# Hybrid decoder step on one core: the output weights' sums split over three places, and the sample rows' products moved

## The chip, the cores and the metric

The kernel runs on one core of a Trainium2 chip. The engines named here are PE (TensorE, matrix products), DVE (VectorE), ACT (ScalarE), POOL (GpSimd) and SP (SyncE, which issues nearly all the DMAs of this kernel, in the order of its queue). The metric is the device time of one execution in microseconds (us); three runs of the kernel before took 834.67, 834.83 and 835.5 us, with the median 834.83.

## The reference

One layer of a decoder, applied to a prompt of 1024 rows of width 1024 and to 8 x 4 sample rows with their caches and states. Two branches read the same normalised input h: a matrix memory (mLSTM, 4 heads of 128) and a windowed attention with sinks (8 heads of 64). The branches are gated, projected, merged, projected once more, and added to x; a last RMSNorm ends it. What matters here is its end:

```python
def layer(x, c, C0, n0, m0, k_past, v_past, w_ada, b_ada, g_norm, w_in, ..., w_mo, w_ao, w_o):
    h, gate = adaln_in(x, c, w_ada, b_ada, g_norm)
    (mq, mk, mv, mi, mf, mo, mz, aq, ak, av, az, gm, ga) = split_in(h @ w_in)
    y_m, C, n, m = mlstm_branch(mq, mk, mv, mi, mf, mo, mz, C0, n0, m0, b_i, b_f, g_mn)
    ...
    y_a = o.astype(x.dtype) * jax.nn.silu(az)
    u = jax.nn.sigmoid(gm) * (y_m @ w_mo) + jax.nn.sigmoid(ga) * (y_a @ w_ao)
    x = x + gate * (u @ w_o)

y_prompt = rmsnorm(yp, g_final)
y_sample = rmsnorm(ys, g_final)
```

The other outputs are the new states and caches. w_o is the tensor w_out of the kernel; gate is one vector of 1024 for the whole prompt, so the kernel multiplies the columns of w_out by it once and leaves it out of the product of the prompt's rows.

## The kernel before

**Products.** A product in fp32 is made as three matmuls of a faster format: each operand is split into a high part (a cast, on ACT) and a low part (operand minus high part, on DVE), and `mm` (line 275) issues hi x hi, hi x lo and lo x hi. In the names a tile with h at its end, or wh, is a high part; l or wl is a low part. Large products are made by Strassen's scheme: two by two blocks, seven products of sums of blocks instead of eight. The sums are DVE work, and a split follows each.

**Stages.** The input and the projections; from about 205 to 650 us the 18 pairs of `block_products` (4 `head_in`, 8 `gate`, 2 `query_gate`, 4 `head_gate`, each pair seven products of two blocks); the attention's output product (tiles wl_ao.., ax, ay, u_h); the heads' output product `mem_out` (tiles g_w_mo, eight steps d of three pieces each, about 692 to 741 us); the output rows (four blocks of 256 rows, seven products each, tiles foX, foZ, foW and foY in PSUM); and a short tail. In a block of rows the products come in the order 1, 5, 6, 2, 7, 3, 4.

**Side work.** Beside the pairs run generators: the sample rows' heads, the prompt's heads, and `out_weights` (line 1964). They are held by a planner (`Side`) whose clock `side.now` is advanced by each matmul's estimated time; a generator yields a lag, and is stepped again when the clock has passed it. What a step issues goes to its engine's queue at that place. Each engine works its queue in order, so this planner and the order of the code set what stands ahead of what. In the output rows the order is that of the code.

**The output weights.** `out_weights` starts in the sixth pair. For each K tile of KA = (0, 1, 4, 5) it loads four raw tiles of w_out (wor), multiplies them by the gate (gb), makes the seven operands b11, b21, b22, t1, t2, t3, t4 of Strassen's scheme, splits each (wosh on ACT, wosl on DVE) and stores both parts to DRAM (woD). In `mem_out` the 28 pairs of parts are loaded again (wo_b11h, wo_b11l and so on, 256 KB each) by `weights_out`.

**The samples' last head.** Beside the `head_gate` pairs the last sample head ends in a chain of small DVE instructions, a reciprocal (fsden), a root by Newton steps (fsv, fsr_y, fsr_w) and a scaled tile sz. PE transposes sz into sty, and DVE makes gs of it.

**w_mo.** Each step d of `mem_out` needs the weight tile w_mo of that d: loaded by `preload` (wr_w_mo), split by ACT (wh_w_mo) and DVE (wl_w_mo). Behind a piece of PE's, DVE takes the result with a gate tile: tgw_mo<-tgw_mo,g_w_mo, then u_h or u_l<-u,tgw_mo. The splits of d + 1 are issued in the middle of the step d.

**The sample rows.** `sample_rows` is a generator that the output loop steps by `aside(...)`, which names the blocks in which that place takes a step. Its product of 32 sample rows with w_out is made in four groups of four small matmuls (tile fo in the profile, fo8_0 and fo8_1 in the code), each group reading four raw tiles of w_out that stand in rows_l and rows_h. The loads of the first group are issued ahead of the first product, behind g_final, gsD (the samples' gate, loaded twice into the same tile) and two tiles of x_prompt.

Of the kernel before, what the change touches and what calls it, by code (L numbers as in the profile page):

```python
# [24 lines left out]
NS = NB * NT  # L25
# [148 lines left out]
def body(tc, a):  # L174
    nc = tc.nc
    with ExitStack() as ctx:
# [17 lines left out]
        def ht(shape, name, dt=F32):  # L194
            return sp.tile(shape, dt, tag="half", bufs=50, name=name)
# [58 lines left out]
        def dma(out, in_, late=False):  # L254
            stores(in_.tensor)
            issue(out, in_, late)
# [1446 lines left out]
        def att_products():  # L1703
# [26 lines left out]
            for j, (n, i) in enumerate(flat):  # L1730
# [9 lines left out]
                if i == 3 and n == 2:  # L1740
                    split(ymD, *ymx, PCOLS, 0)
                if i == 2 and not nxt:
                    for d in range(2):
                        preload(("w_mo", d))
                split_ahead(j + 2)
                if i == 3 and not nxt:
# [216 lines left out]

        def out_weights():

            gb = [ht([128, 512], f"gb2{f}") for f in range(2)]
            for f in range(2):
                dma(gb[f], gbD[:, HALF[f]].to_broadcast((128, 512)))

            def keep(n, k, t):  # L1970
                parts = [ht([128, 512], f"wos{x}", F32R) for x in "hl"]
                S.copy(parts[0], t)
                V.tensor_tensor(parts[1], t, parts[0].bitcast(F32), op=ALU.subtract)
                woD[n, k] = [dp.tile([128, 512], F32, name=f"woD{n}{k}{x}") for x in "hl"]
                for d, x in zip(woD[n, k], parts):
                    due.append((side.now + 4.0, d, x.bitcast(F32)))

            for k in KA:
                raws = []
                for kk in (k, k + 2):  # L1980
                    for f in range(2):
                        raws.append(ht([128, 512], f"wor{k}{f}"))
                        dma(raws[-1], a["w_out"][kk * 128:(kk + 1) * 128, HALF[f]])
                yield 10.0, ""
                for j, t in enumerate(raws):
                    with not_before(V):
                        V.tensor_tensor(t, t, gb[j % 2], op=ALU.mult)
                    yield 2.4, ""
# [4 lines left out]
                yield WLAG, ""  # L1993
                V.tensor_tensor(b12, b12, b11, op=ALU.subtract)
                keep("t1", k, b12)
                yield WLAG, ""
                keep("b11", k, b11)
                yield WLAG, ""
                V.tensor_tensor(b11, b11, t3, op=ALU.add)
                keep("t2", k, b11)  # L2000
                yield WLAG, ""
                keep("t3", k, t3)
                yield WLAG, ""
                keep("b21", k, b21)
                yield WLAG, ""
                V.tensor_tensor(b21, b21, b11, op=ALU.subtract)
                keep("t4", k, b21)
                yield WLAG, ""

        KA, WLAG = (0, 1, 4, 5), 4.0  # L2010
        pairs = [Pair(head_in, i) for i in range(len(paired))] + [Pair(gate, d) for d in range(KT)] + [Pair(query_gate, i) for i in range(2)] + [Pair(head_gate, h) for h in range(NH)]

        def hook(n, i):
            if n == 0 and i in (6, 5):
                side.until(lambda: {6: "t2", 5: "t1"}[i] in formed)
            if i == 6:
                if pairs[n].kind is query_gate:
                    side.until(lambda: len(units_done) == 16)
                side.until(lambda: len(samples_done) >= {head_in: 0, gate: 0, query_gate: 1, head_gate: pairs[n].i + 2}[pairs[n].kind])
            if (n, i) == (OUT_WEIGHTS, 6):  # L2020
                side.add("g", out_weights())
            if (n, i) in LOADS:
                side.add("x", att_sums(LOADS.index((n, i))))
# [22 lines left out]
        for _ in att:  # L2046
            pass
        side.finish("x")
        banks[:] = [pg, pg, pa, pa]
        class Rows:  # L2050

# [26 lines left out]
            def product(self, n, o, first, c0=0, w=512):  # L2078
                hi, lo = self.w[n]
                for k in range(4):  # L2080
                    bh, bl = (t[:, c0:c0 + w] for t in wo[OPERANDS[n]][k])
# [5 lines left out]
        wo = {n: [] for n in ("b11", "b21", "b22", "t1", "t2", "t3", "t4")}  # L2087
# [8 lines left out]
        def weights_out(n):  # L2096
            for _ in range(n):
                n, k = wo_parts.pop(0)
                aside = len(wo_parts) < 8
                hi = ht([128, 512], f"wo_{n}h", F32R)  # L2100
                lo = granule(f"wo_{n}l", "wr", 9, F32R).rearrange("p k n -> p (k n)") if aside else ht([128, 512], f"wo_{n}l", F32R)
                for t, d in zip((hi, lo), woD[n, k]):
                    dma(t.bitcast(F32), d, True)
                wo[n].append((hi, lo))
# [50 lines left out]
        def sample_rows():  # L2155
# [14 lines left out]
            for f in range(2):  # L2170
# [34 lines left out]
        for i, r in enumerate(blocks_of_rows):  # L2205
# [35 lines left out]
            def seventh():  # L2241
# [114 lines left out]
```

## Time and profile before

| | us |
|---|---|
| median of three runs (834.67 to 835.5) | 834.83 |
| the profiled execution | 833.81 |
| its span in the profile | 832.0 |
| PE busy | 805.9 (97%) |
| DVE busy | 604.6 (73%) |
| ACT busy | 417.9 (50%) |
| POOL busy | 47.5 (6%) |

A row of a timeline gives the start, the duration, the engine, the line, the operation, then what is written and what is read by the program's names (without buffer numbers), shapes, and in brackets how long the engine stood idle before it and for what. Lines 220, 261, 275 and 280 are helpers through which all the work goes, so the tile names tell the places. A list of waits gives who waited for whom: total, times, longest. Durations of neighbouring rows overlap a little, since instructions are pipelined: two rows of 0.67 on DVE start 0.6 apart, and matmuls with 512 columns last 0.39 and start 0.23 apart. A row of windows gives the window, its length, the busy time of PE, PE's weight loads, DVE, ACT and POOL with their instruction counts, PE's granted clock (1.00 is full), the mean share of the DMA engines and GB/s. The mean granted clock of the whole execution is 0.995.

### The profile page before, as it was taken

How to read it: one execution, taken by the hardware profiler on the slowest of the kernel's cores; microseconds unless marked ns; L12 is line 12 of the kernel's file. 1: busy time of each engine (PE TensorE's matmuls, PEld its weight loads, DVE VectorE, ACT ScalarE, POOL GpSimd, SP SyncE). 2: the span in 40 equal slices, each digit the busy share in tenths (PEclk: the TensorE clock that was granted, in tenths of full speed). 3: DMA queues.
4: the chain of work that ended last, by engine and by line, in shares of the span. 5: the costliest groups of instructions: out<-in, count | busy, mean ns of one | idle time of the engine just before them, and what ended most of it. 6: DMA issues, size and time to landing. Idle time of an engine off the chain costs nothing.

```text
span 832.0 us, 15086 instructions
## 1 busy us (share of the span) xinstructions
PE 805.9 (97%) x5105; PEld 666.3 (80%) x5105; DVE 604.6 (73%) x1503; ACT 417.9 (50%) x1019; POOL 47.5 (6%) x111
## 2 busy tenths in 40 slices
PE   6999999999999999999999999998999999999996
PEld 3779797888788788888888778886888789987775
DVE  4889886747646456476656997999568996565887
ACT  5664366556455564555655555445346652014433
POOL 0120000000000001000001001101002101000000
PEclk9999999999999999999999999999999999999998
DMA  9995657446535325537756667768536789766632
GB/s 335 371 318 160 224 180 219 155 163 194 177 123 192 130 73 170 184 100 263 246 172 216 220 217 233 250 202 274 169 94 187 240 308 380 283 209 209 203 108 107
DMA packets 116481, 171.79 MB, mean 206 GB/s; under 512 B 21536, under 2 KB 55456, under 8 KB 116372
## 3 DMA queue, kind: packets, MB, share of 16 engines
q1 hardware_dynamic: 110756, 160.08, 58.2%
q10 hardware_dynamic: 4176, 6.56, 2.1%
q0 software_dynamic: 1472, 4.20, 1.4%
q8 instruction: 40, 0.66, 0.3%
q14 instruction: 37, 0.30, 0.1%
HBM read 118.13 MB, written 53.67 MB: 206 GB/s over the span
## 4 chain that ended last, share of the span: by engine, by line
PE 80%; DVE 11%; DMA 3%; issue 3%; ACT 2%; SPq 1%; DVEq 0%; ACTq 0%
PE bx L275 11%; PE bw L275 10%; PE by L275 10%; PE g_w_mo L275 6%; PE bz L275 5%; PE g_mq L275 3%; PE g_aq L275 3%; PE foX L275 2%; PE sc L275 2%; PE oT L275 2%; PE smp L275 2%; PE pt L280 2%; PE foW L275 2%; PE n L275 2%; PE g_mv L275 1%
## 5 line engine op out<-in xcount | busy, mean ns | idle before, releaser
L220 ACT ACTIVATE p<-p,nmx 128x256 f32<-128x256 f32 (+1 forms) x64 | 31.0, 486 | 18.7 <-DVE nmx L220 18.4
L275 PE MATMUL g_w_mo<-ym_l,wl_w_mo 128*128 128x384 f32 (+1 forms) x96 | 31.1, 324 | 2.4 <-DVE wl_w_mo L220 2.4
L275 PE MATMUL g_aq<-h_h,wh_aq 128*128 128x384 f32 (+1 forms) x96 | 32.2, 336 | 0.0
L275 PE MATMUL g_aq<-h_h,wl_aq 128*128 128x384 f32 (+1 forms) x96 | 30.9, 322 | 0.0
L275 PE MATMUL g_aq<-h_l,wh_aq 128*128 128x384 f32 (+1 forms) x96 | 30.8, 321 | 0.0
L275 PE MATMUL g_w_mo<-ym_l,wh_w_mo 128*128 128x384 f32 (+1 forms) x96 | 30.8, 321 | 0.0
L275 PE MATMUL g_w_mo<-ym_h,wh_w_mo 128*128 128x384 f32 (+1 forms) x96 | 30.8, 321 | 0.0
L220 DVE CUSTOM_DVE_ANT_0 p<-sc,cst,sink 128x256 f32<-128x256 f32 (+1 forms) x64 | 26.1, 462 | 5.3 <-PE sc L275 5.2
L220 DVE SCALAR_TENSOR_TENSOR tgw_mo<-tgw_mo,g_w_mo 128x384 f32<-128x384 f32 (+1 forms) x24 | 12.5, 520 | 19.7 <-PE g_w_mo L275 18.2
L275 PEld LDWEIGHTS g_w_mo<-ym_l,wl_w_mo 128*128 128x128 f32 x96 | 18.0, 188 | 3.4 <-DVE wl_w_mo L220 3.4
L275 PEld LDWEIGHTS g_aq<-h_h,wh_aq 128*128 128x128 f32 x96 | 18.0, 188 | 2.6 <-issue 1.5
L220 DVE TENSOR_TENSOR et<-et,S 128x384 f32<-128x384 f32 (+1 forms) x12 | 6.1, 509 | 19.2 <-PE S L275 16.4
L261 POOL DMA_DIRECT2D oD<-uqv x16 | 8.8, 552 | 184.3 <-ACT uqv L220 171.0
L220 DVE TENSOR_TENSOR wosl<-wor,wosh 128x512 fp32r<-128x512 f32 x24 | 16.5, 686 | 3.7 <-ACT wosh L220 3.0
L275 PE MATMUL sc<-ukv,uqv 64*128 64x256 f32 (+1 forms) x128 | 18.0, 390 | 0.7 <-DMA ukv<-kD 0.6
L275 PEld LDWEIGHTS g_w_mo<-ym_l,wh_w_mo 128*128 128x128 f32 x96 | 18.0, 188 | 0.0
L275 PEld LDWEIGHTS g_w_mo<-ym_h,wh_w_mo 128*128 128x128 f32 x96 | 18.0, 188 | 0.0
L275 PEld LDWEIGHTS g_aq<-h_l,wh_aq 128*128 128x128 f32 x96 | 18.0, 188 | 0.0
L275 PEld LDWEIGHTS g_aq<-h_h,wl_aq 128*128 128x128 f32 x96 | 18.0, 188 | 0.0
L220 ACT CAST wh_w_mo<-wr_w_mo 128x512 fp32r<-128x512 f32 x8 | 4.9, 622 | 26.1 <-DMA wr_w_mo<-w_mo 17.1
L220 DVE COPY p<-pt 128x512 f32<-128x512 f32 (+1 forms) x16 | 10.5, 655 | 10.3 <-PE pt L280 10.3
L220 ACT CAST wosh<-wor 128x512 fp32r<-128x512 f32 x24 | 14.9, 621 | 4.8 <-DVE wor L220 2.0
(1961 smaller groups left out, 2831.3 us busy)
## 6 DMA issues: line engine op xcount, KB each, us to landing
x<-xT SPq DMA_DIRECT2D x16, 256.0 KB
early_h<-w_ada SPq DMA_DIRECT2D x8, 512.0 KB
adar_ga<-w_ada SPq DMA_DIRECT2D x16, 256.0 KB
wr_ga<-w SPq DMA_DIRECT2D x16, 256.0 KB
wr_gm<-w SPq DMA_DIRECT2D x16, 256.0 KB
taD<-gt SPq DMA_DIRECT2D x16, 256.0 KB
tmD<-gt SPq DMA_DIRECT2D x16, 256.0 KB
wor<-w_out SPq DMA_DIRECT2D x16, 256.0 KB
```

The lines of the kernel that those rows point to most:

```text
L220: ins = f(*args, **kw)
L261: ins = (eng or nc.sync).dma_start(out, in_)
L275: in_order(nc.tensor.matmul(out, lhsT, rhs, start=start, stop=stop, skip_group_check=more))
L280: in_order(nc.tensor.transpose(out, in_, idn))
```

## The change

It has five parts.

1. `out_weights` treats the K tiles by place. Tiles 0 and 1 are made beside the heads as before. Tile 4 waits until the second `head_gate` pair has begun and, before it multiplies, until all the sample heads are done; its lags are 3.0 and not 4.0. Tile 5 waits until all the heads are finished, is made inside `mem_out`, and its parts stay on chip (`wo[n][5] = parts`): they are neither stored nor loaded.
2. `weights_out` loads 21 pairs of parts and not 28, on another schedule: (3, 3, 3, 2, 2, 1, 0, 0) behind the steps of `mem_out`, seven at the end. `out_weights` is finished in the last step of `mem_out` and not ahead of the first.
3. Four tiles of w_mo are loaded ahead of `mem_out` and not two, and each step d loads d + 4.
4. `sample_rows` multiplies its sums by the gate in the step in which they are added, with one yield fewer.
5. In the output loop the step behind product 6 is now taken in blocks 0, 1 and 2 and not only 1 and 2, and the step behind product 2 is gone.

```diff
@@ att_products
-                    for d in range(2):
+                    for d in range(4):
                         preload(("w_mo", d))
@@ out_weights
                 S.copy(parts[0], t)
                 V.tensor_tensor(parts[1], t, parts[0].bitcast(F32), op=ALU.subtract)
+                if k == KA[-1]:
+                    wo[n][k] = parts
+                    return
...
             for k in KA:
+                lag = WLAG
+                if k in KA[2:]:
+                    while len(begun) < k - 3:
+                        yield 1.0, ""
+                    lag = 3.0
+                if k != KA[1]:
+                    gb = [ht([128, 512], f"gb2{f}") for f in range(2)]
+                    for f in range(2):
+                        dma(gb[f], gbD[:, HALF[f]].to_broadcast((128, 512)))
...
                 yield 10.0, ""
+                while k == KA[2] and len(samples_done) < NH + 1:
+                    yield 0.5, ""
@@ hook
+            if n == len(pairs) - NH + 1 and not begun:
+                begun.append(4)
...
         side.finish("x")
+        begun.append(5)
@@ output weights and mem_out
-        wo_parts = [(n, k) for n in ("b11", "t1", "t2", "b21", "t3", "b22", "t4") for k in KA]
+        wo_parts = [(n, k) for n in ("b11", "t1", "t2", "b21", "t3", "b22", "t4") for k in KA[:3]]
...
-        side.finish("g")
         for d in range(KT):
             if d == KT - 1:
+                side.finish("g")
                 row_start()
+            elif d < KT - 4:
+                preload(("w_mo", d + 4))
             mem_out(d, ymx, u, row_start if d == KT - 1 else None)
-            if d < 6:
-                weights_out((4, 4, 4, 3, 3, 3)[d])
+            weights_out((3, 3, 3, 2, 2, 1, 0, 0)[d])
         weights_out(len(wo_parts))
@@ sample_rows
                     V.tensor_tensor(sums[f], acc[f][j:j + 32], sums[f], op=ALU.add)
-                yield
+                V.tensor_tensor(sums[f], sums[f], gsb[:NS, HALF[f]], op=ALU.mult)
+            yield
             for f in range(2):
-                V.tensor_tensor(sums[f], sums[f], gsb[:NS, HALF[f]], op=ALU.mult)
                 V.tensor_tensor(xb[:NS, HALF[f]], xb[:NS, HALF[f]], sums[f], op=ALU.add)
@@ the output loop
-            aside(1, 2)
+            aside(0, 1, 2)
             for c in range(2) if i else ():
                 rows_out(2 * i - 2 + c, before[0][c], rs[:, c:c + 1])
             row_start()
             r.product(2, X, False)
             add_row(xb[0], lo, X)
-            aside(1, 2)
             square(xb[0][:, lo], ss[:, 0:1])
```

How this moves instructions is seen in the engines' queues. First DVE, beside the `head_gate` pairs, where the last sample head's chain from fsden to sz stands; wosl and wor are the output weights' sums, wl_phead_gate and wr_mo the pairs' own. Before:

```order
L220 SCALAR_TENSOR_TENSOR fsden<-sz 32x2
L220 TENSOR_TENSOR wl_phead_gate_7__6973<-wr_mz_0_6649,wh_phead_gate_7__6972 128x512
L220 SCALAR_TENSOR_TENSOR zt<-zt,ztz 128x512
L220 TENSOR_TENSOR wosl<-wor_6487,wosh 128x512
L220 TENSOR_TENSOR zt<-zt,ho 128x512
L220 SCALAR_TENSOR_TENSOR zt<-zt,by 128x512
L220 TENSOR_TENSOR wr_mo_1_6647<-wr_mo_1_6647,wr_mo_0_6645 128x512
L220 TENSOR_TENSOR zt<-zt,ho 128x512
L220 TENSOR_TENSOR fsden<-fsden,fls 32x2
L220 TENSOR_TENSOR wor_6487<-wor_6487,wot_6770 128x512
L220 RECIPROCAL fsden<-fsden 32x2
```

And now, from the same instruction on:

```order
L220 SCALAR_TENSOR_TENSOR fsden<-sz 32x2
L220 TENSOR_TENSOR zt<-zt,ho 128x512
L220 TENSOR_TENSOR fsden<-fsden,fls 32x2
L220 RECIPROCAL fsden<-fsden 32x2
L220 TENSOR_TENSOR wl_phead_gate_7__6854<-wr_mz_0_6567,wh_phead_gate_7__6853 128x512
L220 SCALAR_TENSOR_TENSOR zt<-zt,by 128x512
L220 TENSOR_TENSOR fsv<-fsden 32x2
L220 TENSOR_TENSOR zt<-zt,ho 128x512
L220 TENSOR_TENSOR fsv<-fsv,sssq 32x2
L220 TENSOR_SCALAR fsv<-fsv 32x2
```

Between the first fsden and sz stood 40 instructions, 21 of them 128x512 and six of these of the output weights; now there are 21, five of them 128x512 and none of the output weights.

Second, DVE in `mem_out`, around the split wl_w_mo of the step d = 6. Before, it stands behind the taking of the last piece of the step before:

```order
L220 SCALAR_TENSOR_TENSOR tgw_mo_1_8535<-tgw_mo_1_8535,g_w_mo_8629 128x384
L220 TENSOR_TENSOR u_h_7755<-u_h_7755,tgw_mo_0_8533 128x384
L220 TENSOR_TENSOR u_h_7755<-u_h_7755,tgw_mo_1_8535 128x384
L220 SCALAR_TENSOR_TENSOR tgw_mo_2_8537<-tgw_mo_2_8537,g_w_mo_8644 128x288
L220 TENSOR_TENSOR wl_w_mo_0_8609<-wr_w_mo_0_8543,wh_w_mo_0_8608 128x512
```

Now it stands behind the first piece of the step d = 3, with the gate's multiplication of the kept K tile (wor<-wor,gb) near it:

```order
L220 TENSOR_TENSOR u_l_7687<-u_l_7687,tgw_mo_2_8267 128x288
L220 SCALAR_TENSOR_TENSOR tgw_mo_0_8333<-tgw_mo_0_8333,g_w_mo_8413 128x384
L220 TENSOR_TENSOR wl_w_mo_0_8549<-wr_w_mo_0_8331,wh_w_mo_0_8548 128x512
L220 TENSOR_TENSOR u_l_7687<-u_l_7687,tgw_mo_0_8333 128x384
L220 TENSOR_TENSOR wor_8206<-wor_8206,gb_8197 128x512
L220 SCALAR_TENSOR_TENSOR tgw_mo_1_8335<-tgw_mo_1_8335,g_w_mo_8429 128x384
```

The split has moved ahead by two steps and a half, and every split behind it likewise.

Third, PE in the first block of output rows, at the sample rows' first group (fo_0). Before, it stands between product 3 (foW<-wo_b22) and product 4 (foY<-wo_t4):

```order
L275 MATMUL foW<-wo_b22h,u0wh_8870 128x512
L275 MATMUL foW<-wo_b22l,u0wh_8870 128x512
L275 MATMUL foW<-wo_b22h,u0wl_8871 128x512
L275 MATMUL fo_0_8824<-rows_l_8811,u_h_7755 32x512 x2
L275 MATMUL fo_0_8824<-rows_h_8812,u_l_7756 32x512 x2
L275 MATMUL foY_8886<-wo_t4h,u0wh_8889 128x512
```

Now it stands between product 6, whose last matmuls read the kept tile's parts (wosh, wosl) from where they were made, and product 2 (foX<-wo_b21):

```order
L275 MATMUL foW<-wosl,u0wh_8769 128x512
L275 MATMUL foW<-wosh,u0wl_8770 128x512
L275 MATMUL foY_8838<-wo_b11h,u0wh_8769 128x512
L275 MATMUL fo_0_8776<-rows_l_8763,u_h_7686 32x512 x2
L275 MATMUL fo_0_8776<-rows_h_8764,u_l_7687 32x512 x2
L275 MATMUL foX<-wo_b21h,u0wh_8784 128x512
```

The group has moved ahead of three products. SP's queue around the loads that it reads has kept its order: the last parts, g_final, gsD twice, x_prompt, w_out.

More of the change, by code (lines that the diff above doesn't have):

```diff
@@ L1964, in out_weights @@
         def out_weights():
-            gb = [ht([128, 512], f"gb2{f}") for f in range(2)]
-            for f in range(2):
-                dma(gb[f], gbD[:, HALF[f]].to_broadcast((128, 512)))
             def keep(n, k, t):
@@ L1987, in out_weights @@
                         V.tensor_tensor(t, t, gb[j % 2], op=ALU.mult)
-                    yield 2.4, ""
+                    yield min(2.4, lag), ""
                 b11, b12, b21, b22 = raws
@@ L1992, in out_weights @@
                 keep("b22", k, b22)
-                yield WLAG, ""
+                yield lag, ""
                 V.tensor_tensor(b12, b12, b11, op=ALU.subtract)
                 keep("t1", k, b12)
-                yield WLAG, ""
+                yield lag, ""
                 keep("b11", k, b11)
-                yield WLAG, ""
+                yield lag, ""
                 V.tensor_tensor(b11, b11, t3, op=ALU.add)
                 keep("t2", k, b11)
-                yield WLAG, ""
+                yield lag, ""
                 keep("t3", k, t3)
-                yield WLAG, ""
+                yield lag, ""
                 keep("b21", k, b21)
-                yield WLAG, ""
+                yield lag, ""
                 V.tensor_tensor(b21, b21, b11, op=ALU.subtract)
                 keep("t4", k, b21)
-                yield WLAG, ""
+                yield lag, ""
         KA, WLAG = (0, 1, 4, 5), 4.0
+        begun = []
+        wo = {n: {} for n in ("b11", "b21", "b22", "t1", "t2", "t3", "t4")}
         pairs = [Pair(head_in, i) for i in range(len(paired))] + [Pair(gate, d) for d in range(KT)] + [Pair(query_gate, i) for i in range(2)] + [Pair(head_gate, h) for h in range(NH)]
@@ L2080, in product @@
                 for k in range(4):
-                    bh, bl = (t[:, c0:c0 + w] for t in wo[OPERANDS[n]][k])
+                    bh, bl = (t[:, c0:c0 + w] for t in wo[OPERANDS[n]][KA[k]])
                     mm(o, hi[:, k], bh, start=(first and k == 0), stop=False, more=not first)
@@ L2086, in body @@
         blocks_of_rows = [Rows(i) for i in range(4)]
-        wo = {n: [] for n in ("b11", "b21", "b22", "t1", "t2", "t3", "t4")}
-        wo_parts = [(n, k) for n in ("b11", "t1", "t2", "b21", "t3", "b22", "t4") for k in KA]
+        wo_parts = [(n, k) for n in ("b11", "t1", "t2", "b21", "t3", "b22", "t4") for k in KA[:3]]
         order_out = [(i, n) for i in range(4) for n in ((1, 5, 6, 2, 7, 3, 4) if i < 3 else (1, 5, 6, 2, 3, 7, 4))]
@@ L2103, in weights_out @@
                     dma(t.bitcast(F32), d, True)
-                wo[n].append((hi, lo))
-        side.finish("g")
+                wo[n][k] = hi, lo
         for d in range(KT):
             if d == KT - 1:
+                side.finish("g")
                 row_start()
+            elif d < KT - 4:
+                preload(("w_mo", d + 4))
             mem_out(d, ymx, u, row_start if d == KT - 1 else None)
-            if d < 6:
-                weights_out((4, 4, 4, 3, 3, 3)[d])
+            weights_out((3, 3, 3, 2, 2, 1, 0, 0)[d])
         weights_out(len(wo_parts))
```

## The prediction

> **What bounds the kernel now.** I read four views in this order: engine shares, TensorE's (PE's) waits, the windows and timelines around each wait, then the queue of SP, on which the loads stand.
>
> ```profile
> PE 805.9 (97%) x5105; PEld 666.3 (80%) x5105; DVE 604.6 (73%) x1503; ACT 417.9 (50%) x1019; POOL 47.5 (6%) x111
> ```
> ```profile
> PE sty L280 <- DVE sz L220: 4.2, 1, 4.2
> PE g_w_mo L275 <- DVE wl_w_mo L220: 2.4, 3, 0.8
> ```
>
> PE is the bound at 97%, so the time is PE's work plus its waits, and the change takes no matmul away. Behind 400 us only two waits are worth a microsecond. The first lies in the gate stage, the second is three equal ones in the heads' output product.
>
> The first wait, on PE and by windows (the column after POOL's is the granted clock):
>
> ```profile
> 581.58 0.60 PE L280 MATMUL sty<-cst,sz 104*128 104x104 f32 x2 [4.15 <-DVE sz L220]
> 581.88 0.78 PE L275 MATMUL bx<-h_h,wh_phead_gate__6995 128*128 128x512 f32 x1
> ...
> 586.15 0.40 PE L275 MATMUL bw<-h_h,wh_phead_gate__7052 128*128 128x512 f32 x1
> ```
> ```profile
> 583.00:584.00 1.00, 1.00 (x4) 0.81 (x3) 0.00 (x0) 0.00 (x0) 0.00 (x0) 0.50 1.01 299
> ```
>
> The wait costs more than its 4.15 us. The 12 matmuls of bx take 581.88 to 586.15, 4.27 us; at full rate 15 of this kind start in 3.42 us (741.60 to 745.02, further down), 0.228 each, so 12 take 2.73. The clock stands at 0.50 behind the wait, and that is 1.5 us more: together 5.65.
>
> What VectorE (DVE) does meanwhile, from the first instruction of the chain that ends in sz:
>
> ```profile
> 566.74 0.14 DVE L220 SCALAR_TENSOR_TENSOR fsden<-sz 32x2 f32<-32x2 f32 x1
> ...
> 568.01 0.67 DVE L220 TENSOR_TENSOR wosl<-wor,wosh 128x512 fp32r<-128x512 f32 x1
> ...
> 580.31 0.69 DVE L220 TENSOR_TENSOR wor<-wor,wor 128x512 f32<-128x512 f32 x1
> ...
> 581.10 0.59 DVE L220 TENSOR_SCALAR sz<-sz,fsden,fsr_y 32x128 f32<-32x128 f32 x2
> ```
>
> The chain's own small instructions alternate with 21 of 128x512; six of those are the output weights' sums of the last K tile (the first and the last of the six are shown). DVE has no idle time in the stretch, so sz is as late as the queue ahead of it is long.
>
> **The change, term by term.** Durations are from the profiled execution: 833.81 us, span 832.0, 1.02 below the median of the runs, 834.83. I sum against 833.81 and carry the difference to the median.
>
> *The sums leave the sz chain.* In the new order five 128x512 instructions stand between fsden and sz, and 16 small ones. From 566.74 that is about 5 x 0.6 + 16 x 0.2 + 0.6 for sz, so sz is ready near 573.6, almost four microseconds before PE comes for it at 577.4 (581.58 less the 4.15). The wait and its half clock go: -5.65. If only the six sums went and the other 15 stayed, sz would come 3.6 us earlier and the gain would still be 3.6 plus the clock, 5.1; that is the lower end. Late next there is nothing: PE's next operands were made ahead.
>
> *The w_mo splits move ahead.* Two rows of DVE, the window with two of the waits, two rows of PE:
>
> ```profile
> 728.16 0.46 DVE L220 SCALAR_TENSOR_TENSOR tgw_mo<-tgw_mo,g_w_mo 128x288 f32<-128x288 f32 x1
> 728.53 0.68 DVE L220 TENSOR_TENSOR wl_w_mo<-wr_w_mo,wh_w_mo 128x512 fp32r<-128x512 f32 x1
> ```
> ```profile
> 720.00:730.00 10.00, 8.40 (x52) 7.76 (x52) 6.19 (x13) 0.62 (x1) 0.00 (x0) 1.00 0.39 127
> ```
> ```profile
> 728.13 0.34 PE L275 MATMUL g_w_mo<-ym_h,wh_w_mo 128*128 128x384 f32 x1
> 729.27 0.45 PE L275 MATMUL g_w_mo<-ym_l,wl_w_mo 128*128 128x384 f32 x1 [0.80 <-DVE wl_w_mo L220]
> ```
>
> The split stands behind a tgw_mo which needs the last piece of the previous d, so PE waits for it at each of three d. Start to start it is 1.14 where a matmul of 384 columns takes 0.17 to 0.19, so 0.95 is lost each time, 2.85 in all. With four tiles loaded ahead and each split a d or more earlier, all three go: -2.85, at least the 2.4 listed. The two more loads go to SP's queue ahead of the tgw_mo loads, which are read only when a first piece is done: 0.
>
> *One K tile moves to the last head pairs.* That is 4 multiplications, 4 adds and 7 splits on DVE, 15 x 0.6 = 9 us, at 590 to 631. Windows there and behind (behind the window's length stand the busy times of PE, its weight loads, DVE, ACT and POOL, then clock, DMA share and GB/s), then a split on DVE and its use on PE:
>
> ```profile
> 590.00:600.00 10.00, 10.00 (x46) 8.26 (x44) 6.90 (x11) 4.53 (x9) 0.00 (x0) 1.00 0.27 93
> 600.00:610.00 10.00, 10.00 (x72) 8.24 (x72) 5.97 (x12) 3.78 (x8) 0.00 (x0) 1.00 0.21 68
> 610.00:620.00 10.00, 10.00 (x45) 8.26 (x44) 7.14 (x12) 4.45 (x8) 0.00 (x0) 1.00 0.51 161
> 620.00:630.00 10.00, 10.00 (x73) 8.24 (x72) 6.12 (x12) 4.05 (x9) 1.28 (x1) 1.00 0.59 169
> 630.00:640.00 10.00, 10.00 (x45) 8.27 (x45) 9.88 (x13) 6.78 (x13) 2.84 (x2) 1.00 0.37 116
> ```
> ```profile
> 656.99 0.41 DVE L220 TENSOR_TENSOR wl_ao0C<-wr_ao,wh_ao0C 128x256 fp32r<-128x256 f32 x1
> ...
> 658.34 0.40 PE L275 MATMUL ay<-yat3h,wl_ao0C 128*128 128x512 f32 x1
> ```
>
> DVE is free for 13.9 of the 40 us to 630, which covers the nine; ACT and the DMA engines are at 0.6 or less. But DVE is full from 630 on, and there a split is ready 0.9 us before its use (657.40 against 658.34). The last sums stand just ahead of that stretch; one or two of 0.6 us pushed into it cost 0 to 2 us. I take +0.5, near the low end, since the free time ahead is larger than the work. Fourteen stores move with it, onto a queue with room.
>
> *One K tile stays on chip, inside the output product.* Its 15 DVE instructions, 7 ACT casts and 6 loads lie beside 49 us of matmuls, and 14 stores and 14 loads of 256 KB go. No gain from the transfers: no wait there is for one. At the join to the output rows (T, PE's first foX) there is a cost. The rows of before, on PE and on DVE:
>
> ```profile
> 741.60 0.39 PE L275 MATMUL foX<-wo_b11h,u0wh 128*128 128x512 f32 x1
> ...
> 745.02 0.39 PE L275 MATMUL foZ<-wo_t1h,u0wl 128*128 128x512 f32 x1
> ```
> ```profile
> 743.20 0.68 DVE L220 TENSOR_TENSOR u0wl<-us,u0wh 128x512 fp32r<-128x512 f32 x1
> ```
>
> u0wl ended at T+2.28 and was needed at T+3.42. Now the last sum's split and two adds stand ahead of it: about T+3.6, so PE waits 0.2: +0.2 (0 to 0.6).
>
> *The sample rows' products move forward on PE.* These four small matmuls (fo<-rows, u) stood behind the sixth of the first block's seven products; now they stand behind the third, ahead of foX<-wo_b21h. They need four tiles of w_out. Both places on PE, SP's queue, and windows of its transfers:
>
> ```profile
> 750.23 0.39 PE L275 MATMUL foX<-wo_b21h,u0wh 128*128 128x512 f32 x1
> ...
> 758.48 0.62 PE L275 MATMUL fo<-rows_l,u_h 128*32 128x512 f32 x2
> ```
> ```profile
> 743.54 5.72 SPq L261 DMA_DIRECT2D rows_l<-gsD  x2
> 749.31 0.42 SPq L261 DMA_DIRECT2D rows_l<-x_prompt  x1
> 749.78 0.42 SPq L261 DMA_DIRECT2D rows_h<-x_prompt  x1
> 750.25 0.90 SPq L261 DMA_DIRECT2D rows_l<-w_out  x2
> 751.20 0.94 SPq L261 DMA_DIRECT2D rows_h<-w_out  x2
> ```
> ```profile
> 752.00:753.00 1.00, 1.00 (x6) 0.81 (x6) 0.05 (x1) 0.50 (x1) 0.00 (x0) 1.00 0.99 389
> ...
> 756.00:757.00 1.00, 1.00 (x6) 0.84 (x5) 0.86 (x2) 0.11 (x1) 0.00 (x0) 1.00 0.68 260
> 757.00:758.00 1.00, 1.00 (x6) 0.81 (x5) 0.00 (x0) 1.00 (x3) 0.00 (x0) 1.00 0.06 23
> ```
>
> Before, PE came to them at T+16.9 and the transfers were over near 757.4, T+15.8: hidden by 1.1 us. Now PE comes after three products and two seeding matmuls, at 750.23 or T+8.63, and with the 0.2 at T+8.8. The loads do not come earlier with it. On SP's queue ahead of them stand the last weight parts, g_final, two loads of gsD and 1 MB of x_prompt; the second gsD waits for the first one's landing (the 5.72 us), so x_prompt was issued at T+7.7, and from there to the end of the traffic 8.1 us passed. In the new order the last part but one waits for a DVE add that now ends near T+2.3, and the four issues up to gsD bring its start from T+1.94 to about T+3.8. As part of the traffic is then already moved, I take 1.5 of these 1.8 us: x_prompt at T+9.2, the w_out tiles at T+17.3. PE waits 17.3 - 8.8 = 8.5 us, with four products of the block queued behind. Lower end 7.0 (loads no later than before), upper 9.6 (the full shift and a landing 0.8 after the last byte).
>
> The clock after a wait that long: the only one of over 4 us in this half of the trace cost 1.5 more, and the three of 0.8 left it at 1.00. So +1.5 (0 to 1.7). [...]
>
> The later halves of these products get their loads when the first are read, three products (8.2 us) ahead, with nothing queued before them: 0. The product with the gate that follows the sums moves a step earlier on DVE, two small rows in the second block: 0.
>
> Sum: -5.65 - 2.85 + 0.5 + 0.2 + 8.5 + 1.5 = +2.2. On the median 834.83 that is 837.0; two gains are paid away by one new wait.
>
> **The rivals.** *The loads come in time.* One thing decides, when the first gsD lands: each microsecond that x_prompt is issued earlier is one less of PE's wait. Without the sample wait and its clock the sum is -7.8 (827.0). A wait of 6.3 with the 1.5 brings it to zero, which is w_out at T+15.1 and gsD landed by T+7.0; below 3 the clock may stay up too, and the time is under 830. For it: each of these loads waits for nothing but the queue, and fourteen transfers fewer are read in the output product. Against it: T+7.7 was reached before, with the queue free from T+1.9.
>
> *The loads run at the full rate.* The 2.1 MB of x_prompt and w_out took 8.1 us, the end of it at 260 GB/s; at the 389 of the window at 752 they take 5.4, w_out is there at T+14.6, the wait is 5.8 and the time 834.3. Against it: the same loads did not do so before, with nothing else on the queue. [...]
>
> *DVE's backlog reaches PE.* Ahead of 660 the splits have 0.9 us to spare; if the moved sums come there, or the fourteen stores delay a load of that stage, PE waits 2 to 4 us where I have 0.5: 838.5 to 840.5. For it: the full window from 630 on. Against it: the idle 13.9 us ahead.
>
> *The wait for sz stays*, if the chain is held by something other than the queue (a PE result that a zt in it reads): 5.65 are not gained, 842.6. Against it: DVE shows no idle between fsden and sz.
>
> **How the numbers follow.** My sum has 0.5, by its small terms from 835.3 to 838.5; the loads in time 0.2 (827 to 834); the full rate 0.07; the backlog 0.18; the wait for sz 0.05. About 0.2% (1.7 us) is what a measurement of this kernel can tell from no change: faster is below 833.2, slower above 836.5. Faster is the first rival but for its upper edge, and a little of the second: 0.2. Same is the rest of both and 0.15 of my own case: 0.22. All else, 0.58, is slower. The range leaves out the lower half of the first rival and the last one: 829.5 to 841.
>
> **What the changed profile would show.** The list of PE's waits has no sty and no g_w_mo on wl_w_mo; instead fo on DMA rows_h<-w_out, 7 to 9.5 us, right behind foY's seed, with windows of clock 0.5 after it. SP's timeline has gsD's pair at about 5 us and x_prompt near T+9. If fo waits under 6 us, or the list still has sz, or att_sums waits for its wl splits for over 2 us, I am wrong at that term.

## The result, and the profile after

The changed kernel takes 840.24 us, the median of four runs (839.70 to 841.93); the kernel before took 835.16 beside it (four runs, 834.67 to 836.01). The ratio is 1.0063, with a 95% interval of 1.0046 to 1.0081: slower by 5.1 us. The profiled execution took 841.93 us, span 840.1. It was the slowest of its four, and the profiled one of before, 833.81, lay under its median, so that the two profiles lie 8.1 us apart: 3.0 us of that is the choice of executions. The sums below are taken from the two profiles.

The busy times of the engines did not move by more than 2.6 us; what changed are PE's waits, and the rate at which it works behind them. The page's line of busy times and the list of PE's waits behind 400 us:

```profile
PE 808.5 (96%) x5105; PEld 665.6 (79%) x5105; DVE 605.7 (72%) x1503; ACT 417.8 (50%) x1019; POOL 46.4 (6%) x111
```
```profile
PE fo L275 <- DMA rows_l<-w_out: 8.6, 1, 8.6
PE foY L275 <- DVE rows_h L220: 1.9, 2, 1.7
PE ay L275 <- DVE wl_ao0D L220: 1.1, 1, 1.1
PE by L275 <- DVE hg1z L220: 1.1, 1, 1.1
PE aw L275 <- ACT aw L220: 0.5, 1, 0.5
```

sty and g_w_mo have left the list. So have two waits of 0.4 in the sample heads (smp and ty, near 480 us). In their place stand five that before were smaller or not there at all. In the order of time:

**The gate stage.** DVE's chain and PE's use of it, in the timeline of after:

```profile
563.67 0.14 DVE L220 SCALAR_TENSOR_TENSOR fsden<-sz 32x2 f32<-32x2 f32 x1
...
569.62 0.59 DVE L220 TENSOR_SCALAR sz<-sz,fsden,fsr_y 32x128 f32<-32x128 f32 x2
```
```profile
576.43 0.34 PE L280 MATMUL sty<-cst,sz 104*128 104x104 f32 x2
576.55 0.47 PE L275 MATMUL bx<-h_h,wh_phead_gate__6876 128*128 128x512 f32 x1
```

From fsden to sz it is now 6 us and not 14.4; sz is there 6.2 us before PE comes, and bx starts at the full rate (the clock is 1.00 from 570 to 580).

**The last head pairs and the attention's output product.** DVE's windows where one K tile's sums were put (busy times of PE, its weight loads, DVE, ACT, POOL, then clock, DMA share and GB/s), and behind them PE's two waits with the DVE instruction that ends each:

```profile
590.00:600.00 10.00, 10.00 (x73) 8.21 (x73) 7.31 (x15) 4.48 (x10) 0.00 (x0) 1.00 0.25 80
600.00:610.00 10.00, 10.00 (x46) 8.28 (x45) 9.53 (x16) 5.39 (x10) 0.00 (x0) 1.00 0.54 189
610.00:620.00 10.00, 10.00 (x73) 8.21 (x73) 6.51 (x14) 4.70 (x10) 0.00 (x0) 1.00 0.86 271
620.00:630.00 10.00, 10.00 (x45) 8.05 (x44) 8.78 (x13) 6.21 (x13) 2.21 (x2) 1.00 0.93 302
```
```profile
641.81 0.50 PE L275 MATMUL by<-t4h,wh_phead_gate__7580 128*128 128x512 f32 x1 [1.10 <-DVE hg1z L220]
...
658.85 0.50 PE L275 MATMUL ay<-yat4h,wl_ao0D 128*128 128x512 f32 x1 [1.12 <-DVE wl_ao0D L220]
```
```profile
641.08 0.67 DVE L220 TENSOR_TENSOR hg1z<-p,by 128x512 f32<-128x512 f32 x1
...
658.39 0.41 DVE L220 TENSOR_TENSOR wl_ao0D<-wr_ao,wh_ao0D 128x256 fp32r<-128x256 f32 x1
```

The 40 us hold 32.1 us of DVE's work, where before they held 26.1: six of the nine moved microseconds (two of the fifteen moved instructions stand just ahead of 590). And 7.9 us stay idle there: DVE waits for ACT (3.7 us in all), for PE (1.4), and once for a load:

```profile
614.87 0.43 DVE L220 TENSOR_TENSOR ws<-wr_ao 128x256 f32<-128x256 f32 x1 [2.72 <-DMA wr_ao<-w_ao]
```

In the kernel before, DVE waits for no load in these 40 us. Now SP issues stores of tile 4's parts (woD) among the loads, and the DMA share from 610 to 630 is 0.86 to 0.93 where it was 0.51 to 0.59. What did not fit is carried past 630, where DVE is full.

**The join of the output rows.** PE at the sample rows' group, the group's weight loads (PEld), SP's queue of the loads that it reads, and the windows of their transfers:

```profile
753.05 1.92 PE L275 MATMUL fo<-rows_l,u_h 128*32 128x512 f32 x3 [8.64 <-DMA rows_l<-w_out]
...
756.87 0.80 PE L275 MATMUL foX<-wo_b21h,u0wh 128*128 128x512 f32 x1
```
```profile
753.05 0.18 PEld L275 LDWEIGHTS fo<-rows_l,u_h 128*32 128x32 f32 x2 [9.06 <-DMA rows_l<-w_out]
753.77 0.18 PEld L275 LDWEIGHTS fo<-rows_l,u_h 128*32 128x32 f32 x2 [0.53 <-DMA rows_l<-w_out]
754.40 0.18 PEld L275 LDWEIGHTS fo<-rows_h,u_l 128*32 128x32 f32 x2 [0.46 <-DMA rows_h<-w_out]
755.03 0.18 PEld L275 LDWEIGHTS fo<-rows_h,u_l 128*32 128x32 f32 x2 [0.44 <-DMA rows_h<-w_out]
```
```profile
739.91 6.70 SPq L261 DMA_DIRECT2D rows_l<-gsD  x2
746.67 0.41 SPq L261 DMA_DIRECT2D rows_l<-x_prompt  x1
...
747.60 0.90 SPq L261 DMA_DIRECT2D rows_l<-w_out  x2
```
```profile
743.00:744.00 1.00, 1.00 (x6) 0.83 (x5) 0.00 (x0) 0.00 (x0) 0.00 (x0) 1.00 1.06 401
...
745.00:747.00 2.00, 0.00 (x0) 0.00 (x0) 0.00 (x0) 1.37 (x3) 0.00 (x0) 1.00 0.02 4
...
749.00:752.00 3.00, 0.00 (x0) 0.00 (x0) 0.75 (x2) 0.00 (x0) 0.00 (x0) 0.50 0.93 351
...
753.00:758.00 5.00, 4.95 (x11) 1.66 (x12) 0.83 (x2) 0.00 (x0) 0.00 (x0) 0.50 0.54 186
```

PE's first foX (T) is at 735.28, 6.3 us earlier than before, and this is what all parts ahead of it are worth. At 744.4 PE stops for 8.64 us. The second load of gsD holds the queue until the first has landed (SP waits 5.7 us of the pair's 6.70 for it), behind 400 GB/s of weight parts; then there is nothing on the DMA engines for over two microseconds, and x_prompt goes out at 746.67. Behind the wait the clock stands at 0.50 for five microseconds more, and the small group takes 3.8 us (753.05 to 756.87), where before it took 1.1. Not all of that is the clock. The 8.64 us end with the first of the four w_out tiles. The weight loads show that PE waits for each of the other three in turn, and the last is there only at 755.03 (T+19.8), 2.0 us behind the first; from there to the next product it is 1.84 us.

**The third block of rows.** DVE, then PE's use:

```profile
800.10 2.13 DVE L220 TENSOR_TENSOR fo8s<-fo,fo8s 32x512 f32<-32x512 f32 x3
802.26 0.68 DVE L220 TENSOR_TENSOR fo8s<-fo8s,rows_l 32x512 f32<-32x512 f32 x1
802.87 2.72 DVE L220 SCALAR_TENSOR_TENSOR rows_h<-rows_h,fy,rows_l 128x512 f32<-128x512 f32 x4
...
808.87 0.68 DVE L220 TENSOR_TENSOR rows_h<-rows_h,foY 128x512 f32<-128x512 f32 x1
```
```profile
809.69 0.47 PE L275 MATMUL foY<-wo_t4h,u2wh 128*128 128x512 f32 x1 [1.66 <-DVE rows_h L220]
```

Three of the sample rows' sums and their multiplication with the gate, 2.8 us, now stand ahead of the finished rows' four multiplications; the add that frees foY is late behind both.

The two profiles side by side, by PE's starts, with the terms of the forecast:

| us | forecast | profiles |
|---|---|---|
| the wait for sz and its half clock | -5.65 | -5.8 |
| the waits for wl_w_mo | -2.85 | -3.25 |
| DVE's backlog behind the head pairs | +0.5 | +3.6 |
| u0wl at the join | +0.2 | +0.3 |
| fo's wait for w_out (forecast: the last tile; profile: the first) | +8.5 | +8.7 |
| behind it (forecast: the half clock; profile: the other three tiles too) | +1.5 | +3.4 |
| foY's waits in the later blocks | 0 | +1.4 |
| smp and ty | 0 | -1.1 |
| where the projections begin | | +0.3 |
| sum | +2.2 | +7.6 |

PE's last matmul stands 7.7 us later than before (831.93 against 824.23), so the table leaves 0.1 open; 0.4 more lies behind that matmul.

### The profile page after: what moved, and what is told of

Read it like the earlier page. It is cut to its first block, busy times and chain, and to the rows that moved or that the text cites. A ratio compares the mean times of both kernels' runs of the same rounds, so it can differ in the third digit from the quotient of the medians.

```text
span 840.1 us, 15038 instructions
## 1 busy us (share of the span) xinstructions
PE 808.5 (96%) x5105; PEld 665.6 (79%) x5105; DVE 605.7 (72%) x1503; ACT 417.8 (50%) x1019; POOL 46.4 (6%) x111
## 5 line engine op out<-in xcount | busy, mean ns | idle before, releaser
L220 DVE CUSTOM_DVE_ANT_0 p<-sc,cst,sink 128x256 f32<-128x256 f32 (+1 forms) x64 | 26.1, 463 | 5.3 <-PE sc L275 5.2
L220 DVE SCALAR_TENSOR_TENSOR tgw_mo<-tgw_mo,g_w_mo 128x384 f32<-128x384 f32 (+1 forms) x24 | 12.4, 518 | 10.2 <-PE g_w_mo L275 9.6
L220 DVE COPY p<-pt 128x512 f32<-128x512 f32 (+1 forms) x16 | 10.5, 654 | 10.3 <-PE pt L280 10.3
L220 ACT ACTIVATE sq<-rows_h 128x512 f32<-128x512 f32 (+2 forms) x14 | 8.1, 579 | 19.0 <-issue 14.4
```

The lines of the kernel that those rows point to most:

```text
L220: ins = f(*args, **kw)
```

## The experiments

My theory after the result: the samples' products, moved ahead of their loads, cost all of the loss, and the rest of the change gains about 7 us. The rivals: something else in the change eats the gains; and, on the loads, that x_prompt's place in the queue does or does not set the wait.

**The sample rows as before, all else as in after.**

```diff
             for f in range(2):
                 for j in (32, 64, 96): ...
-                V.tensor_tensor(sums[f], sums[f], gsb[:NS, HALF[f]], op=ALU.mult)
-            yield
+                yield
             for f in range(2):
+                V.tensor_tensor(sums[f], sums[f], gsb[:NS, HALF[f]], op=ALU.mult)
...
-            aside(0, 1, 2)
+            aside(1, 2)
...
             add_row(xb[0], lo, X)
+            aside(1, 2)
```

> The changed kernel with parts 4 and 5 undone: the sample rows' first group stands behind product 3 again, as in the kernel before. My theory (the wait for w_out and the slow clock behind it are the whole loss in the output rows): fo's wait of 8.6 us goes, with it the 2.7 us of the group at half clock and 0.75 of the next product, some 12.0 us together, and perhaps the 2.0 of foY's new waits for rows_h: 840.2 - 12 to 14 = 826 to 828. The rival (the first block is late for its operands, since the u0wl splits stand behind late x_prompt tiles on DVE, and the wait only moves): PE waits instead for u0wl or rows_h, and the time stays over 834.

Measured: 832.01 us (eight runs, 830.21 to 833.57) against 834.80; ratio 0.9966 (0.9953 to 0.9978). The move of the samples thus costs 8.2 us, and turns a gain into a loss. But what is left is a gain of 2.8 and not of 7 to 9. A wait that was hidden stands in the open, the one that my rival named. PE's waits, and DVE at that place:

```profile
PE foW L275 <- DVE u0wl L220: 2.6, 1, 2.6
```
```profile
750.16 0.69 DVE L220 TENSOR_TENSOR rows_l<-rows_l,foZ 128x512 f32<-128x512 f32 x1 [7.66 <-DMA rows_l<-x_prompt]
...
751.97 1.28 DVE L220 TENSOR_TENSOR u0wl<-u_l,u0wh 128x512 fp32r<-128x512 f32 x2
```

x_prompt was issued at 745.33, T+10.3 with T at 735.02, against T+7.7 before. The add that needs it keeps DVE from its queue for 7.66 us, with the splits u0wl behind it, and for these PE waits. In after this wait is covered by the longer one for w_out. In the profiled execution (830.73) the clock stayed up behind it (1.00 from 752 to 756). The mean granted clock of the eight executions is 0.997 or 0.998 in four of them, the profiled one included, and 0.993 to 0.995 in the other four. So it seems to have fallen in half of them, which are slower by 1.8 us in the mean (832.7 against 830.9).

**The move of the samples alone**, in the kernel before (the same edit, the other way round).

```diff
-            aside(1, 2)
+            aside(0, 1, 2)
...
             add_row(xb[0], lo, X)
-            aside(1, 2)
```

> The kernel before with parts 4 and 5 alone: only the sample rows' steps moved. My theory: the loads are where they were, x_prompt at T+7.7 and w_out at T+15.8 to 16.5, PE comes at T+8.6, so fo waits 7 to 8 us, plus 3.4 of slow clock, plus 0 to 2 for foY: 835.2 + 10.5 to 13 = 845.5 to 848. The rival (the wait comes from the later queue of SP that the kept K tile brings): fo waits under 3 us and the time is under 839.

Measured: 845.36 us (845.26 to 846.11) against 834.80, ratio 1.0132 (1.0117 to 1.0147): slower by 10.6, at the lower edge of what I expected. PE's waits and SP's queue:

```profile
PE fo L275 <- DMA rows_l<-w_out: 5.8, 1, 5.8
...
PE foY L275 <- DVE rows_h L220: 1.9, 2, 1.7
```
```profile
744.23 6.02 SPq L261 DMA_DIRECT2D rows_l<-gsD  x2
750.29 0.42 SPq L261 DMA_DIRECT2D rows_l<-x_prompt  x1
```

The wait is there without any of the other parts, 5.75 us of it with x_prompt at T+8.0. I had 7 to 8 for it: my T+15.8 to 16.5 was meant for all four tiles, and by the weight loads the last is there at 758.78, T+16.5, 1.95 us behind the first. The remaining 2.9 us of after's 8.64 go with x_prompt's later issue. The wait of foY for rows_h is there too, 1.7, so it comes of the sample rows' steps (parts 4 and 5).

**The samples' gate loaded once** (the second load of gsD left out; the values in the tile are the same), else as in after.

```diff
         lo, hi = HALF
-        dma(gsb[:NS], gsD)
         row_start()
```

> The changed kernel with gsD loaded once and not twice, so that x_prompt does not wait for a landing. By the prediction's own words (each microsecond of x_prompt's issue is one of PE's wait) x_prompt is issued some 6 us earlier and fo waits 2 to 3 us, the clock stays up: 830 to 833. The rival (the transfers ahead fill the DMA engines until 744.5, and only the idle stretch from 744.6 to 747.2 is saved): fo waits near 6 us, the clock falls all the same, 837 to 838.

Measured: 836.99 us (836.90 to 838.63) against 834.80, ratio 1.0033 (1.0020 to 1.0046). PE and SP's queue:

```profile
749.68 1.92 PE L275 MATMUL fo<-rows_l,u_h 128*32 128x512 f32 x3 [5.01 <-DMA rows_l<-w_out]
```
```profile
740.19 0.34 SPq L261 DMA_DIRECT2D rows_l<-x_prompt  x1
```

x_prompt goes out 6.5 us earlier than in after, and the wait is shorter by only 3.6. The rival holds: the listed wait is 5.0 us, and 6.9 up to the last tile (751.60), the clock falls all the same (0.50 from 749 to 750), and the time is 837. The loads stand behind the weight parts on the DMA engines, which have no empty stretch now (a share of 0.97, 1.05 and 1.01 in the three 5 us from 735 to 750). What the duplicate load costs is about the stretch in which nothing moved, the 2.6 us up to 747, and one more; the rest stays, with the DMA engines full (364 to 377 GB/s from 742 to 750).

**Tile 4 beside the heads as before**, only tile 5 on chip, on top of the first experiment.

```diff
-                if k in KA[2:]:
+                if k == KA[3]:
                     while len(begun) < k - 3:
...
-                if k != KA[1]:
+                if k not in KA[1:3]:
...
-                while k == KA[2] and len(samples_done) < NH + 1:
-                    yield 0.5, ""
```

> As the first of these (parts 4 and 5 undone), and K tile 4 beside the heads as in the kernel before, with only tile 5 kept on chip. My theory (tile 4 in the last head pairs pushes DVE's backlog into the attention's output product, 3.0 us in the waits of by for hg1z, aw and ay for wl_ao0D): these go, the chain to sz stays clear since no sum of tile 5 stands in it, and the small waits of smp and ty come back (1.1): 1.5 to 3 us under the first of these, 823.5 to 826. The rival (tile 4 beside the heads delays sz again, as tile 5 did): sty waits over 2 us and the time is that of the first or above.

Measured: 829.81 us (829.59 to 830.28) against 834.80, ratio 0.9946 (0.9929 to 0.9962), 2.2 under the first experiment, as its backlog would have it. PE's waits:

```profile
PE foW L275 <- DVE u0wl L220: 3.1, 1, 3.1
PE smp L275 <- ACT gts L220: 0.4, 1, 0.4
...
```

by, ay and aw are gone, so they were the moved tile's, and so is DVE's wait for the load of w_ao; smp and ty (0.4 each) are back, so their loss came with it. sty is not back: taking one K tile out of the heads already clears the chain to sz. The absolute time stays above what I expected, because the expectations of these two runs did not have the wait for u0wl. In this run it is 3.06 us, and the clock fell to half behind it (a mean of 0.66 from 750 to 755), for about 1.7 us more (PE's starts from that wait to the foY behind the samples' group, against the same starts in the run of the best together, where neither is).

**The loads of w_mo ahead, alone**, in the kernel before.

```diff
-                    for d in range(2):
+                    for d in range(4):
                         preload(("w_mo", d))
...
+            elif d < KT - 4:
+                preload(("w_mo", d + 4))
```

> The kernel before with part 3 alone: four tiles of w_mo loaded ahead, each step loading d + 4. My theory: the three waits of g_w_mo for wl_w_mo (0.95 each) go and nothing takes their place: 834.8 - 2.85 = 832. The rival (DVE or the DMA queues of the output product are full, and the earlier loads push back the weight parts or x_prompt, so that the gain is given back at the join): 834 to 835.

Measured: 830.56 us (830.12 to 831.41) against 834.86, ratio 0.9951 (0.9938 to 0.9963): 4.3 us, where I had 2.85. g_w_mo no longer stands among the waits, and from the first g_w_mo to the first foX PE needs 45.94 us and not 49.19, 3.25 less. About a microsecond of the gain does not lie in that stage: 0.6 of it is the choice of executions, since the two profiled ones differ by 3.7 and not 4.3, and the rest lies ahead of the stage, where this edit changes nothing that I can name. x_prompt goes out at T+7.6 here (745.60, T at 737.99), as before; with tile 5 on chip beside it, in the run above, at T+10.8. So the kept tile makes it late, with the schedule of the loads (part 2) that came with it; no run here tells these two apart.

**The best of these together**: tile 5 on chip, w_mo ahead, the samples as before, gsD once.

```diff
         lo, hi = HALF
-        dma(gsb[:NS], gsD)
         row_start()
```

> The fourth experiment's kernel (samples' steps as before, tile 4 beside the heads, tile 5 kept on chip) with gsD loaded once. My theory: foW's wait of 3.1 us for u0wl stands behind the late x_prompt on DVE; x_prompt issued without the landing comes 3 to 4 us earlier, so the wait and the slow clock behind it (1.9 by the profile) go: 829.8 - 3 to 5 = 825 to 827. The rival (x_prompt is held by the transfers ahead, and DVE is full): foW still waits over 1.5 us and the time is 828 or more.

Measured: 824.42 us (824.14 to 825.40) against 834.86, ratio 0.9877 (0.9864 to 0.9891), 0.6 under what I expected. It beats the kernel before by 10.4 us and the changed one by 15.8. SP's queue, and all of PE's waits behind 400 us that are worth listing:

```profile
736.23 0.34 SPq L261 DMA_DIRECT2D rows_l<-x_prompt  x1
```
```profile
PE smp L275 <- ACT gts L220: 0.4, 1, 0.4
PE foY L275 <- DVE rows_h L220: 0.4, 1, 0.4
PE ty L280 <- ACT smps L220: 0.4, 1, 0.4
```

With T at 731.53, x_prompt goes out at T+4.7, and the wait for u0wl is gone with it. So the late x_prompt was its cause: only the duplicate load was taken away between these two kernels.

**The changed kernel once more**, for how much its waits vary.

> The changed kernel once more, for a second profiled execution: what differs between executions of the same program. My theory: every wait is the same to 0.3 us (fo 8.6, foY 1.7, by 1.1, ay 1.1), and only the length of the half clock behind fo's wait differs, 3 to 6 us of it, which moves the time by 1 to 2 us; the median is 839.5 to 841. The rival (the waits themselves differ by a microsecond or more, since the transfers vary): fo's wait is under 7.8 or over 9.4.

Measured: 840.37 us (839.29 to 841.19) against 834.86, ratio 1.0066 (1.0051 to 1.0081). The profiled execution took 840.12.

```profile
750.98 2.35 PE L275 MATMUL fo<-rows_l,u_h 128*32 128x512 f32 x3 [7.25 <-DMA rows_l<-w_out]
```

The wait is 7.25 us here and was 8.64; foY's 1.7 and the backlog's two of 1.1 are the same to 0.1. So this wait for DMA differs by 1.4 us between two executions of one kernel, as the rival had it. Only part of that reaches the time: here the second tile comes 1.3 us behind the first (0.7 in the other profile), so that the last is there at T+19.0 against T+19.8. That is 0.8 of the 1.8 us between the two profiled executions; another 0.7 lies ahead of T.

**Parts and sum.** Alone or nearly so, part 3 is worth -4.3, tile 5 on chip on top of it -0.7 (-5.0 in the fourth run less the -4.3), tile 4's move +2.2, the samples' move +10.6: together +7.8, and the change measures +5.1. The 2.7 between are about the 2.6 us of the wait for u0wl, which the long wait covers; that this is what closes the sum is argued, not shown.

## Why the prediction was right, and where it was not

The direction was right, and so was the reason: two gains are paid away by PE's wait for w_out. The time was 3.2 us too low at the medians, and the table's sum 5.4. Of the 5.4, 3.1 us are DVE's backlog, 2.1 PE's wait for w_out up to its last tile, and 1.4 foY's waits; smp and ty take 1.1 off and the w_mo splits 0.4, and the rest are small. Point by point:

- *The sums leave the sz chain*: -5.65 against -5.8, right. sz was ready at 570.2 in after's time; shifted by the 3.1 us by which the chain itself begins earlier, that is 573.3, where 573.6 was worked out.
- *The w_mo splits*: -2.85 against -3.25 in the stage, right. Alone, the part gains 4.3.
- *One K tile moves to the last head pairs*: the first term that failed. I took +0.5 "since the free time ahead is larger than the work" and named 0 to 2 as its ends; it is 3.6, and the run without the move has none of the three waits. DVE's 13.9 idle microseconds were not all free time: 7.9 stayed idle with more work in the queue, 5.1 of them waits for ACT and PE. The other 2.7 is a wait for a load of w_ao that DVE did not have before, and that goes again when tile 4 goes back beside the heads, so it comes with the moved tile's transfers. I had put these "onto a queue with room". The rival that I gave 2 to 4 us, in which "the fourteen stores delay a load of that stage", was nearer than my term, in size and in reason. How much of the 3.6 is the load's and how much DVE's own work is open.
- *fo's wait for w_out*: the second term that failed, though 8.64 stands beside 8.5. That the two numbers agree is luck: my 8.5 ran to all four tiles (T+17.3), and the listed wait ends with the first (the list names rows_l, where I had named rows_h, the last). The last was there at T+19.8, so the wait for w_out is 8.64 + 1.98 = 10.6 us, above my upper end of 9.6. The step that failed is x_prompt's issue: at T+11.4 and not T+9.2, since the pair of gsD began at T+4.6 and took 6.7 us beside the parts' full traffic. From there to the last tile it took 8.4 us, about the 8.1 that I had. So the rival of faster loads was wrong here; only the first tile, 6.4 us behind x_prompt, looks like it.
- *The hinge*, "each microsecond that x_prompt is issued earlier is one less of PE's wait": wrong. Of 6.5 us, 3.6 came back. The queue ahead was one limit and the DMA engines' traffic the next (a share of 0.97 to 1.05 from 735 to 750). The break-even that I gave, w_out at T+15.1, was not reached either: the run with a single gsD has x_prompt at T+4.7 and no landing to wait for, yet the first tile is there at T+14.2 and the last (751.60) at T+16.1, and it is still slower than the kernel before.
- *The clock after the wait*: right in size, as far as the profiles tell. The table's 3.4 (2.7 in fo's group, 0.7 in foX; 3.0 with the samples alone, 3.65 in the second profile) holds the late tiles too. Behind the last tile the clock stands at half for 3.1 us more in after, and for 2.3 and 2.4 with the samples alone and in the second profile; at half rate that costs at most half of it, an estimate of 1.6, 1.2 and 1.2, beside my 1.5 (0 to 1.7). The rest, about 2 us, is the tiles'. What was wrong is the bound. The upper end of 1.7 was my estimate, and no run shows it as a limit. It is half of 3.4 us, and for 3.4 us the clock is at half behind PE's restart in the kernel before; but it is so for 5.1 in after, and behind the wait for sz with the samples alone for the whole stretch from 581 to 587 (0.50), in which PE is busy for 5.83. So half of 3.4 is no upper end.
- *"a step earlier on DVE, two small rows in the second block: 0"*: wrong, the third term that failed. What moved beside those rows were the three sums ahead of the finished rows' multiplications, and behind both stands the add that frees foY: 1.66 us at one place, the same in all four profiles with that step, 1.4 net.
- *Late x_prompt and DVE*: not in the prediction at all. I followed the late loads to PE's fo and not to DVE's adds, which need x_prompt itself; in after the longer wait hides it, and it is worth 5 us as soon as the samples go back (829.81 to 824.42 by the load of gsD alone).
- *smp and ty*: not in the prediction. Two waits of the sample heads go with the moved tile, -1.1.

Open: how much of the 5.1 us belongs to each term at the median, since the terms were measured in single executions, between two of which, of one kernel, the wait for w_out differs by 1.4 us.

## What to carry to other kernels

A consumer whose loads come only just in time gains nothing by being moved ahead in its queue unless the loads are moved too: look for the load that blocks the others (here a tile loaded twice into the same place, whose second load waits 5.7 us for the first to land), and follow each late load to all its readers, on the engines behind them as well. Count an engine's idle time as room only where the work that you add can stand in the queue at that moment, and count the transfers that come with it. Where an instruction group reads several loads, a listed wait may end with the first of them: look at each. And measure the parts of a change alone: here two of them were worth 5 us together, one cost 2 and one 10, and one line beside them was worth another 5.

## What the runs showed of the hardware that was not expected

The half clock did not last equally long in these profiles, not even behind the same wait. Windows narrow enough give its edges, two in the kernel before and two in after:

```profile
581.40:581.60 0.20, 0.02 (x1) 0.05 (x1) 0.20 (x2) 0.20 (x1) 0.00 (x0) 0.88 1.05 389
584.80:585.00 0.20, 0.20 (x2) 0.12 (x2) 0.00 (x0) 0.00 (x0) 0.00 (x0) 0.58 0.85 310
```
```profile
747.50:748.00 0.50, 0.00 (x0) 0.00 (x0) 0.00 (x0) 0.00 (x0) 0.00 (x0) 0.93 0.89 189
758.00:758.50 0.50, 0.50 (x4) 0.41 (x3) 0.00 (x0) 0.00 (x0) 0.00 (x0) 0.83 0.84 242
```

Taken as a mix of 1.00 and 0.50, a mean of 0.88 over 0.2 us is half clock for 0.05 of them, so in the kernel before the clock fell at 581.55, as PE began again (581.58), and was back at 584.97: 3.4 us. In after it fell at 747.93, while PE still waited, and was back at 758.17: 10.2 us, 5.1 of them behind PE's restart. In the same way the windows give 3.4 us for tile 4 beside the heads (0.66 over the five from 750 to 755), 6.9 for gsD once (0.93 over the seven from 742, then 0.50 over one and 0.51 over five) and at least 5.9 for the second profile of after (0.50 over the one from 750, then 0.51 over five). Behind the wait for sz, 4.2 us in three kernels, the clock is at half for 3.4 us in the kernel before (0.66 from 581 to 586), for at least 4.3 with w_mo alone (0.57 in the same five) and for at least 6.0 with the samples alone (0.50 from 581 to 587). It fell for a shorter wait as well: behind one of 3.06 us with tile 4 beside the heads, but not behind one of 2.63 in the profiled execution of the first experiment (1.00 from 752 to 756).

The samples' group looks as if the half clock hit it harder than other matmuls: its eight small matmuls take 1.1 us at full rate and 3.8 behind the wait. The run with tile 4 beside the heads has the same group where the clock is at half for 3.4 of the five us from 750 to 755, with all its tiles there:

```profile
753.66 1.07 PE L275 MATMUL fo<-rows_l,u_h 128*32 128x512 f32 x2
...
755.22 0.50 PE L275 MATMUL foY<-wo_t4h,u0wh 128*128 128x512 f32 x1
```

There it takes 1.56 us. The rest of the 3.8 is the landing of its loads: from the last weight load to the next product it is 1.84 to 1.85 us in all four profiles that have the group behind the wait, and what comes before that is the time between its first and its last tile: 1.93 to 1.98 us in three of them, and 2.58 in the second profile of after, where the whole group takes 4.4.
